# Five instead of four groups of seven-product blocks in the second product of the feed-forward layers, with the third products of three groups moved to the end

## Chip, cores and metric

The kernel runs on one core of one Trainium2 chip. The metric is the time of one execution in device microseconds; less is better. The input is 256 tokens of 1024 channels in float32.

## The reference

The reference is a trunk of two layers. Each layer has a feed-forward network (FFN), a mixer and a second FFN, each with an RMS norm ahead of it and a residual addition behind it:

```python
def swiglu(x, w_in, w_out):
    gate, up = jnp.split(x @ w_in, 2, axis=-1)
    return (jax.nn.silu(gate) * up) @ w_out
...
    for l in range(DEPTH):
        h = h + 0.5 * swiglu(rms_norm(h, ffn1_norm[l]), ffn1_w_in[l], ffn1_w_out[l])
        u = rms_norm(h, mix_norm[l])
        ...
        h = h + merged @ w_out[l]
        h = h + 0.5 * swiglu(rms_norm(h, ffn2_norm[l]), ffn2_w_in[l], ffn2_w_out[l])
    return rms_norm(h, final_norm)
```

The inner width of an FFN is 2816. The second product (by w_out) therefore sums over 22 k tiles of 128 channels, gives 1024 output columns (two halves n of 512) and has 256 tokens (two tiles t of 128). The mixer runs a Mamba-2 branch and a gated DeltaNet branch on one large projection. The change touches the mixer only in how and in what order some matmuls are issued, so the mixer's arithmetic is not shown here.

## The kernel before

**Weights.** All weights stream from HBM as tiles of 128x1024 float32 (512 KB). A tile lands in one of five buffers (`wraw`) by a DMA on SyncE's queue. ScalarE then makes its high part `whi` (line 67, type fp32r) and VectorE the rest `wlo` (line 70). A pair of `whi` and `wlo` is called a form; there are five buffers for each of the two. One float32 product is three matmuls: high by high, high by low, low by high (`mm3`, lines 317 to 320, and `mm3w`, lines 322 to 329). `take()` hands out the next form and issues loads and splits for the ones behind it; with `state["hold"]` set it issues no splits beyond the form that is asked for. The instructions are put in order on each engine at compile time by a scheduler that goes by priority, by readiness in its own model of time, and by free buffers, so an instruction can stand ahead of others that the source has before it. Within an engine the order is then fixed.

**The order of an FFN** is written as a string, `FFN` (line 37). "f" is the first chunk of the first product (four forms, 512-column matmuls). Each "c" is half of one of ten later chunks: two forms and 48 matmuls of 256 columns (`chan_chunk`). After two halves a chunk gives two k tiles of the gated activation: SiLU on ScalarE (tile `sg`), a product on VectorE (`g`), and the split into `gh` and `gl`.

**Block products.** Two k tiles, two token tiles and two column halves make a 2x2x2 block product, which takes seven block products instead of eight if sums of blocks are multiplied. A pair p stands for the k tiles 2p and 2p+1. On the side of the activations `block_sums` makes four sums per pair: four subtractions and additions, two high parts on ScalarE and two rests on VectorE (tiles `sf`, `bsa`, `bsb`, `bsc`, `bsd`). On the side of the weights the sums are made from tiles: `wsum` is loaded on SyncE's queue ("y" in the stream) into one of four slots, a second tile is added to it by an accumulating DMA on GpSimd's queue ("+"), then VectorE adds tiles (q0, q1), then another accumulating DMA follows (q3). `PAIRS` names four groups of two pairs, (1, 2) to (7, 8). "A" in the string is the four products of one group that go to four shared PSUM banks (tiles `p`, forms q1, q0, q2, q3; 24 matmuls). "B" is the three products that go straight to output banks (tiles `o`, forms q4, q5, q6; 18 matmuls). The third of these, q6, multiplies by the group's `wsum` and goes to the bank of token tile 1 and column half 0, so that the slot of the sum stays taken until then. `join` combines the shared banks and adds the results to the residual h by DMA. A "d" in the string is a direct k tile (`DIRECT`: 0, 1, 18 to 21): one form, 12 matmuls. The last five forms of a stage are direct ones, taken with `hold`; their matmuls for token tile 0 come first, so that the norm of that tile can run beside those of tile 1.

**Between stages.** `residual` adds o to h (line 392), `rms_chain` squares and sums on ScalarE (`junk`), takes the power on GpSimd (line 212), scales on VectorE (`hn`, by the norm vector `nw`), transposes on TensorE (`hnT`, line 284), and splits into `uW`, the input of the next stage (tile `t` in the mixer, `f` and `fc` in an FFN). This happens first for token tile 0 and then for tile 1. The norm vector has one buffer, `nw`, loaded by `norm_vec` at the start of an FFN. `out_chunks` multiplies the direct tiles in all three kinds of stages, and `close` ends the mixer with five forms in the same way.

**The cut.** `chan_chunk(ps, cut)` can write its fifth matmul as two of 128 columns (lines 324 to 326). It does so in the first half of the second chunk and in the half chunk after each "A". In the mixer no unit is cut. `ORDER` (lines 45 to 49) gives the order of the mixer's units, k1, k0, q1, k2, k3 first among those here.

## Time and profile before

| | |
|---|---|
| median of 3 runs | 1561.14 us (1560.59 to 1561.25) |
| the profiled execution's own time | 1561.29 us |
| its span | 1559.5 us |
| mean granted TensorE clock | 0.997 |
| busy: PE, DVE, ACT, POOL | 98%, 78%, 61%, 6% of the span |
| PE's share of the chain that ended last | 83% |

In the rows of the profile the start and the duration of instructions are in microseconds from the start of the span. PE is TensorE's matmul side and PEld its weight loads, DVE is VectorE, ACT is ScalarE, POOL is GpSimd, SP is SyncE; "out<-in" are the program's names of the tiles. A row of a window gives busy time with the number of instructions. The four FFNs follow each other at about 10, 602, 788 and 1374 us, and their second products on tiles o begin at 158, 747, 932 and 1519 us.

### The profile page before, as it was taken

To read this page: it belongs to the slowest core of one execution; us is meant where nothing else is said; L and a number is where in the kernel's file an instruction comes from. 1 tells how busy PE (TensorE), PEld (TensorE's weight loads), DVE (VectorE), ACT (ScalarE), POOL (GpSimd) and SP (SyncE) were. 2 spreads that over 40 slices of the span, in tenths; PEclk is the share of its full clock that TensorE was granted. 3 is DMA by queue.
4 is the path that set the end of the run, shared out by engine and by line. 5 is a ranking of instruction groups with operands and counts; after the bars stand their busy time and mean duration, and the time that the engine had idled before them with its cause. 6 is when DMAs were issued, how large, how long until landed. Compare 5 with 4: busy or idle time off the path is not lost.

```text
span 1559.5 us, 29036 instructions
## 1 busy us (share of the span) xinstructions
PE 1533.0 (98%) x11452; PEld 1387.0 (89%) x11452; DVE 1209.6 (78%) x1840; ACT 945.0 (61%) x1534; POOL 95.9 (6%) x108
## 2 busy tenths in 40 slices
PE   8999999999999999999999999999999999999998
PEld 7999879999888888999789998899998888889996
DVE  5778868967899766778677787699579996667786
ACT  5555667766665645556555566686756665455564
POOL 0000110000000000000100011000000000000010
PEclk9999999999999999999999999999999999999999
DMA  8877765553565585577966687655435547856784
GB/s 287 257 251 237 246 213 181 171 163 116 180 207 173 179 255 193 185 251 228 323 209 205 219 257 238 200 188 176 132 123 199 193 161 221 247 173 197 231 251 155
DMA packets 103438, 322.50 MB, mean 207 GB/s; under 512 B 23349, under 2 KB 24325, under 8 KB 102278
## 3 DMA queue, kind: packets, MB, share of 16 engines
q1 hardware_dynamic: 96390, 299.68, 57.0%
q0 software_dynamic: 6912, 20.97, 7.8%
q8 instruction: 90, 1.47, 0.4%
q14 instruction: 46, 0.38, 0.1%
HBM read 314.50 MB, written 1.92 MB: 203 GB/s over the span
## 4 chain that ended last, share of the span: by engine, by line
PE 83%; DVE 7%; DMA 3%; issue 3%; ACT 3%; POOL 1%; SPq 0%; POOLq 0%; ACTq 0%; DVEq 0%
PE fc L329 9%; PE fc L323 9%; PE fc L328 9%; DVE wlo L70 3%; PE t L319 3%; PE t L318 3%; PE t L320 3%; PE b L320 3%; PE b L319 3%; PE b L318 2%; PE o L320 2%; PE o L319 2%; PE o L318 2%; DMA wraw<-in_wst_dram 2%; PE p L319 2%
## 5 line engine op out<-in xcount | busy, mean ns | idle before, releaser
L70 DVE TENSOR_TENSOR wlo<-wraw,whi 128x1024 fp32r<-128x1024 f32 x504 | 611.1, 1221 | 174.5 <-ACT whi L67 166.9
L67 ACT ACTIVATE whi<-wraw 128x1024 fp32r<-128x1024 f32 x504 | 527.1, 1058 | 273.9 <-PE fc L328 87.7
L329 PE MATMUL fc<-uW,wlo 128*128 128x256 f32 x1280 | 354.8, 277 | 0.0
L323 PE MATMUL fc<-uW,whi 128*128 128x256 f32 x1280 | 354.1, 277 | 0.0
L328 PE MATMUL fc<-uW,whi 128*128 128x256 f32 x1260 | 348.2, 276 | 0.0
L323 PEld LDWEIGHTS fc<-uW,whi 128*128 128x128 f32 x1280 | 240.3, 188 | 0.8
L329 PEld LDWEIGHTS fc<-uW,wlo 128*128 128x128 f32 x1280 | 240.5, 188 | 0.0
L328 PEld LDWEIGHTS fc<-uW,whi 128*128 128x128 f32 x1260 | 236.5, 188 | 0.8
L318 PE MATMUL t<-whi,uW 128*128 128x512 f32 x256 | 102.0, 400 | 0.0
L319 PE MATMUL t<-wlo,uW 128*128 128x512 f32 x256 | 100.7, 393 | 0.6 <-DVE wlo L70 0.4
L320 PE MATMUL t<-whi,uW 128*128 128x512 f32 x256 | 100.8, 394 | 0.0
L318 PE MATMUL b<-whi,bh 128*128 128x512 f32 x192 | 76.3, 399 | 0.3 <-ACT bh L67 0.3
L319 PE MATMUL b<-wlo,bh 128*128 128x512 f32 x192 | 74.9, 390 | 0.0
L320 PE MATMUL b<-whi,bl 128*128 128x512 f32 x192 | 74.3, 394 | 0.6 <-DVE bl L70 0.6
L323 PE MATMUL xs<-uW,whi 128*128 128x256 f32 x256 | 72.6, 284 | 0.0
L329 PE MATMUL xs<-uW,wlo 128*128 128x256 f32 x256 | 71.1, 278 | 0.0
L328 PE MATMUL xs<-uW,whi 128*128 128x256 f32 x256 | 70.9, 277 | 0.0
L70 DVE TENSOR_TENSOR wlo<-wsum,whi 128x1024 fp32r<-128x1024 f32 x48 | 58.6, 1221 | 14.7 <-ACT whi L67 13.8
L67 ACT ACTIVATE whi<-wsum 128x1024 fp32r<-128x1024 f32 x48 | 50.8, 1058 | 28.4 <-PE fc L328 23.8
L318 PE MATMUL o<-whi,gh 128*128 128x512 f32 x160 | 63.8, 399 | 1.9 <-ACT whi L67 1.9
L319 PE MATMUL o<-wlo,gh 128*128 128x512 f32 x160 | 63.9, 399 | 1.6 <-DVE wlo L70 1.6
L165 POOL DMA_DIRECT2D wsum<-in_wst_dram x32 | 28.1, 878 | 584.3 <-DVE wlo L70 455.1
(320 smaller groups left out, 3429.8 us busy)
## 6 DMA issues: line engine op xcount, KB each, us to landing
wraw<-in_wst_dram SPq DMA_DIRECT2D x520, 512.0 KB, 5.0
wsum<-in_wst_dram POOLq DMA_DIRECT2D x32, 512.0 KB, 7.3
wsum<-in_wst_dram SPq DMA_DIRECT2D x16, 512.0 KB, 7.1
dc<-rdram SPq DMA_DIRECT2D x8, 1024.0 KB, 9.1
nw<-in_norms_dram SPq DMA_DIRECT2D x6, 512.0 KB, 6.3
h<-u POOLq DMA_DIRECT2D x12, 256.0 KB, 6.8
gb<-rdram SPq DMA_DIRECT2D x8, 256.0 KB, 5.7
h<-in_x_dram SPq DMA_DIRECT2D x4, 256.0 KB, 3.0
```

What stands on the lines that cost most here:

```text
L67: return A.activation(out=o, in_=i, func=func, **kw)
L70: return V.tensor_tensor(out=o, in0=a, in1=b, op=op)
L165: G.dma_start(out=r[:], in_=tile_of(i), accum_op=ALU.add)
L318: PE.matmul(ps, lh, rh, start=start, stop=False)
L319: PE.matmul(ps, lh, rl, start=False, stop=False)
L320: return PE.matmul(ps, ll, rh, start=False, stop=stop)
L323: PE.matmul(ps, wh, mh, start=start, stop=False)
L328: PE.matmul(ps, wh, ml, start=False, stop=False)
L329: PE.matmul(ps, wl, mh, start=False, stop=stop)
```

## The change

The groups become five, (0, 1) to (8, 9), so that 20 of the 22 k tiles are in block products, and the direct tiles are 20 and 21. The string of an FFN becomes "f", four times "cccc" and "A", "cc", "A", "cc", and "BBbbbddeee": "B" is a whole three products, "b" the first two of a group, and "e" the third product of a group whose first two came earlier. The groups take their turn in the order of `LATER`, 4, 0, 1, 2, 3. The fifth "A" comes straight after the chunk that makes pair 9. The sum tile of the fifth group lies in the buffer of the norm vector, which is therefore loaded later, after the first "B". The sums of pairs 8 and 9 lie in free columns of `gh` and `gl`. The k tiles 0 and 1 are copied from PSUM to SBUF ahead of their block sums. At the end come the two direct tiles, first for token tile 0, then for tile 1 with column half 1 ahead of half 0, and then three third products, which all go to tile 1, half 0. The residual addition and the square of tile 1 take half 1 first.

The parts that come from the sibling kernel: the low part of the third form of a next stage is placed behind the last residual addition (`state["late"]`); the five last forms of `close` take the last two k tiles for column half 0 and then for half 1; and the units k1, v2 and x20 of the mixer are cut.

```diff
-FFN = "f" + 8 * "c" + "A" + 4 * "c" + "A" + 4 * "c" + "A" + 2 * "c" + "A" + 2 * "c" + "BdBBBddddd"
-PAIRS = [(1, 2), (3, 4), (5, 6), (7, 8)]
-DIRECT = [0, 1, 18, 19, 20, 21]
+FFN = "f" + 4 * ("cccc" + "A") + "cc" + "A" + "cc" + "BBbbbddeee"
+PAIRS = [(0, 1), (2, 3), (4, 5), (6, 7), (8, 9)]
+LATER = [4, 0, 1, 2, 3]
+DIRECT = [20, 21]
@@ -107,23 +108,19 @@
         o, j2, begun, held = j + 4 * FC, j + 4 * FC + 22, [], []
-        spots, q = [], 0
-        for at, kind in enumerate(FFN):
-            if kind == "A":
-                spots.append(at - 2)
-        o1 = o + FFN[: FFN.index("A")].count("d")
+        later, last = list(LATER), list(LATER[FFN.count("B") :])
+        spots = [at - 2 for at, kind in enumerate(FFN) if kind == "A"]
         for at, kind in enumerate(FFN):
             if at in spots:
-                y = len(stream)
-                stream.extend([("y", o1 + 4 * q), ("+", o1 + 4 * q + 1, y)])
+                y, q = len(stream), len(begun)
+                stream.extend([("n" if q == 4 else "y", o + 4 * (q - len(held))), ("+", o + 4 * (q - len(held)) + 1, y)])
                 begun.append(y)
-                q += 1
             if kind in "fc":
                 j = plan_plain(j, 4 if kind == "f" else 2)
             elif kind == "d":
                 o = plan_plain(o, 1)
             elif kind == "A":
-                y, u = begun.pop(0), len(stream)
+                y, u = begun[len(held)], len(stream)
                 stream.extend([("w", o + 1), ("w", o + 2), ("w", o)])
                 plan.append(("q1", (y, u, u + 1), u + 2))
                 plan.append(("q0", (u + 2, y, u + 1), u + 3))
@@ -132,12 +129,15 @@
                 held.append((y, o + 2))
                 o += 4
             else:
-                y, b22 = held.pop(0)
-                stream.append(("w", b22))
-                plan.append(("q4", (len(stream) - 1,), len(stream)))
-                stream.append(("w", b22 + 1))
-                plan.append(("q5", (len(stream) - 1,), len(stream)))
-                plan.append(("q6", (y,), len(stream)))
+                if kind in "Bb":
+                    y, b22 = held[later.pop(0)]
+                    for i in range(2):
+                        stream.append(("w", b22 + i))
+                        plan.append((f"q{4 + i}", (len(stream) - 1,), len(stream)))
+                else:
+                    y, _ = held[last.pop(0)]
+                if kind in "Be":
+                    plan.append(("q6", (y,), len(stream)))
         return j2
 
     j0 = 0
...
+        elif kind == "n":
+            r = cpool.tile([P, D], F32, tag="nw", name="wsum")
...
                 tt(to, to, by, ALU.add)
+            if i in state["late"]:
+                behind.enter_context(tc.issue_after(state["late"].pop(i).ins))
             tt(lo[:], r[:], f(hi[:]), ALU.subtract)
...
         ss = small([P, 2], "ss")
-        for n in range(2):
+        for n in state["halves"]:
...
                 if add:
-                    add(t)
+                    added = add(t)
...
                 state["behind"][n + 4] = (state["square"].ins, ins.ins)
+                state["late"][n + 2] = added
...
             for t in range(2):
                 order = [(k, n) for n in range(2) for k in range(len(kk))]
                 if t == 1 and not split:
-                    order = [(k, n) for k in range(len(kk)) for n in range(2)]
+                    m = len(kk) - 2 if len(kk) == NSPL else len(kk)
+                    order = [(k, n) for k in range(m) for n in range(2)]
+                    order += [(k, n) for n in range(2) for k in range(m, len(kk))]
...
 
-    def residual(po, nw):
+    def residual(po, nw, first=0):
         def add(t):
-            for n in range(2):
+            state["halves"] = (first, 1 - first) if t == 1 else (0, 1)
+            for n in state["halves"]:
                 hv = h[:, t, n * 512 : (n + 1) * 512]
-                stt(hv, po[t][n][:], 0.5, hv, ALU.mult, ALU.add)
+                ins = stt(hv, po[t][n][:], 0.5, hv, ALU.mult, ALU.add)
+            return ins
...
 
-    def close_blocks(po, stat, sums, pb, nw):
-
-
-
-        direct, joined, n = list(DIRECT), join(pb), 0
-        rest = FFN[FFN.rindex("c") + 1 :]
-        for kind in rest[: len(rest) - NSPL]:
-            if kind == "d":
-                k = direct.pop(0)
-                out_chunks(po, stat, [k], None, first=k == DIRECT[0])
-                continue
+    def close_blocks(po, stat, sums, pb, nxt):
+
+        joined, nw, n_full = join(pb), None, FFN.count("B")
+
+        def third(p):
+            return stat(2 * p + 1, 1)
+
+        for n, q in enumerate(LATER):
             todo = [
-                (po[0][1], lambda p: sums(p, 3), PAIRS[n]),
-                (po[0][0], lambda p: stat(2 * p + 1, 0), PAIRS[n]),
-                (po[1][0], lambda p: stat(2 * p + 1, 1), PAIRS[n]),
+                (po[0][1], lambda p: sums(p, 3), PAIRS[q]),
+                (po[0][0], lambda p: stat(2 * p + 1, 0), PAIRS[q]),
+                (po[1][0], third, PAIRS[q]),
             ]
-            block_products(todo, n == 0, False)
-            n += 1
-            if n % 2 == 0:
+            block_products(todo if n < n_full else todo[:2], n == 0, False)
+            if n == 0 and nxt is not None:
+                nw = norm_vec(nxt)
+            if n < 2:
                 next(joined)
         state["hold"] = True
-        out_chunks(po, stat, direct, direct[-1], group=NSPL, split=nw is None, first=False)
-        return residual(po, nw)
+        ws = [(k, take()) for k in DIRECT]
+
+        def direct(t, n):
+            for k, (wh, wl) in ws:
+                sh, sl = stat(k, t)
+                c = slice(n * 512, (n + 1) * 512)
+                ins = mm3(
+                    po[t][n][:], sh, sl, wh[:, c], wl[:, c],
+                    k == DIRECT[0] and t == n == 1, k == DIRECT[-1] and (t, n) != (1, 0),
+                )
+                state["sums"].append(ins)
+
+        state["sums"] = []
+        for n in range(2):
+            direct(0, n)
+        state["sums"] = []
+        for n in (1, 0):
+            direct(1, n)
+        for q in LATER[n_full:]:
+            state["sums"] += block_products([(po[1][0], third, PAIRS[q])], False, q == LATER[-1])
+        return residual(po, nw, 1)
...
         bsc = slots.tile([P, 4, 2, P], F32R, tag="sI", name="bsc")
-        bsd = s2.tile([P, 2, 2, P], F32R, tag="s2", name="bsd")
+        bsd, bse = (g[2][:, 6:8].rearrange("p i (o t) -> p i o t", o=2) for g in (gl, gh))
...
 
-            q, i = (p - 1) // 2, (p - 1) % 2
+            q, i = p // 2, p % 2
             if j < 3:
                 b = (bsa[:], bsb3)[q % 2]
                 return b[:, i, 0, j, :], b[:, i, 1, j, :]
-            b = (bsc[:, 0:2], bsc[:, 2:4], bsb1, bsd[:])[q]
+            b = (bsc[:, 0:2], bsc[:, 2:4], bsb1, bsd, bse)[q]
...
                             PE.transpose(bank[:, k * S + t * P : k * S + (t + 1) * P], gt[t][:, k * P : (k + 1) * P], ident)
-                    split(0, bank[:].rearrange("p (k t) -> p k t", k=2))
+                    g0 = tmp2("g2")
+                    act(g0[:], bank[:])
+                    split(0, g0[:].rearrange("p (k t) -> p k t", k=2))
+                    block_sums(0, g0)
...
             ps = accb("kk")
-            chan_chunk(ps)
+            chan_chunk(ps, hp == 1)
...
             ps = accb("vv")
-            chan_chunk(ps)
+            chan_chunk(ps, hp == 2)
...
             ps = accb("xs")
-            chan_chunk(ps)
+            chan_chunk(ps, (g, i) == (2, 0))
...
     for l in range(DEPTH):
-        ffn(norm_vec(3 * l + 1))
+        ffn(3 * l + 1)
         mixer(l, norm_vec(3 * l + 2))
-        add = ffn(norm_vec(3 * l + 3) if l + 1 < DEPTH else None)
+        add = ffn(3 * l + 3 if l + 1 < DEPTH else None)
```

8 lines of the change are left out of this document (5 added, 3 removed).

## Prediction

> **What bounds the kernel now.** I read the page first.
>
> ```profile
> span 1559.5 us, 29036 instructions
> PE 1533.0 (98%) x11452; PEld 1387.0 (89%) x11452; DVE 1209.6 (78%) x1840; ACT 945.0 (61%) x1534; POOL 95.9 (6%) x108
> q1 hardware_dynamic: 96390, 299.68, 57.0%
> q0 software_dynamic: 6912, 20.97, 7.8%
> ```
>
> TensorE is busy in 98% of the span, so matmuls set the time, and only fewer matmuls, a faster pace or the removal of the remaining waits can help. The mean duration of a matmul is no price, because matmuls overlap; the price is the length of a row of them. I took the stages of the second product (tiles p and o) by windows and restricted them to their tile. Columns: window, length, then busy time and count of each engine, granted clock, DMA share, GB/s.
>
> ```profile
> core 0: us, PE busy (x) PEld busy (x) DVE busy (x) ACT busy (x), PEclk, DMA share, GB/s
> 659.30:664.76 5.46, 5.43 (x24) 4.36 (x24) 0.00 (x0) 0.00 (x0) 1.00 0.57 103
> 158.18:189.12 30.94, 30.50 (x132) 24.45 (x132) 1.38 (x2) 0.00 (x0) 1.00 0.84 259
> 747.02:784.00 36.98, 33.85 (x132) 26.14 (x132) 1.38 (x2) 0.00 (x0) 0.91 1.01 308
> 932.45:962.38 29.93, 29.91 (x132) 24.62 (x132) 1.38 (x2) 0.00 (x0) 1.00 0.78 240
> ```
>
> Twenty-four matmuls of 512 columns take 5.46 us, so one is worth 0.2275 us. In the third FFN 132 of them on o take 29.93 us, which is the same pace with no wait. The first FFN loses 1.0 us there, and the second loses 7.05 us (36.98 - 29.93) at a DMA share of 1.01. That one stage is the largest wait of the kernel. The DMA issues in it show why:
>
> ```profile
> wraw<-in_wst_dram SPq DMA_DIRECT2D x13, 512.0 KB, 9.5
> wsum<-in_wst_dram SPq DMA_DIRECT2D x4, 512.0 KB, 8.7
> wsum<-in_wst_dram POOLq DMA_DIRECT2D x4, 512.0 KB, 8.9
> ```
>
> Thirteen ordinary weight tiles share the engines with four sum tiles and four accumulating transfers. These sum tiles belong to the next FFN: their four slots come free as the groups finish, and the loads are hoisted into this stage. Weight tiles then land after a median of 9.5 us.
>
> **The change, part by part.**
>
> *Fewer matmuls.* A pair of k tiles costs 24 matmuls directly and 21 as block products. Pairs (0, 1) to (8, 9) replace (1, 2) to (7, 8), that is eight pairs become ten, and six direct tiles become two: 8x21 + 6x12 = 240 matmuls become 10x21 + 2x12 = 234. Six fewer in each of four FFNs are 24 x 0.2275 = 5.4 us off the engine that sets the time: **-5.4 us**.
>
> *The cuts in the mixer.* Matmuls of 256 columns run at two paces. The same five units (k1, k0, q1, k2, k3: 240 matmuls) stand here for layer 0 and then layer 1, and then v2 to the middle of the b units for both layers:
>
> ```profile
> 233.20:261.55 28.35, 28.35 (x242) 28.35 (x242) 25.30 (x54) 20.93 (x37) 0.00 (x0) 1.00 0.59 197
> 1006.12:1033.43 27.31, 27.31 (x242) 27.31 (x242) 24.99 (x54) 20.61 (x36) 0.00 (x0) 1.00 0.61 203
> 307.38:332.30 24.92, 24.92 (x212) 24.80 (x210) 17.60 (x35) 11.18 (x15) 0.00 (x0) 1.00 0.52 139
> 1079.26:1104.20 24.94, 24.94 (x212) 24.80 (x210) 17.88 (x37) 11.49 (x15) 0.00 (x0) 1.00 0.51 141
> ```
>
> Equal work takes 28.35 us and 27.31 us, so 118 ns against 114 ns for one matmul. The v stretches run at 24.92/212 = 118 ns, the slow pace, in both layers. In the FFNs the first chunk after the existing cut runs on at the fast pace. If a cut sets the fast pace here too, k1 is worth 1.04 us in layer 0 and nothing in layer 1 (fast already), and v2 is worth 24.92 x (1 - 27.31/28.35) = 0.9 us in each layer. The cut at x20 precedes only a short stretch, and I put it at 0.1 us in each layer. What a cut costs is seen in the first one of the kernel:
>
> ```profile
> 38.04 0.28 PE L323 MATMUL fc<-uW,whi 128*128 128x256 f32 x1
> ...
> 38.49 0.28 PE L323 MATMUL fc<-uW,whi 128*128 128x256 f32 x1
> ```
>
> Three ordinary starts of 0.118 us would take 0.35 us and these took 0.45 us, so six cuts cost 0.6 us. Sum 1.04 + 1.8 + 0.2 - 0.6: **-2.5 us**; bounds -3.1 and +0.6 (no change of pace).
>
> *Third products kept for the end.* Groups 1 to 3 keep their sum tiles until the five last forms. So of the four slots only that of group 0 is free for the next FFN during this stage, and of the eight extra transfers above about two remain. The next FFN's others move into its own first stage. I take 5.5 of the 7.05 us as saved: **-5.5 us**, bounds -7 and 0. Against it, the stage becomes denser: 132 + 12 matmuls with 18 forms become 114 with 17, and the three "b" groups take two loads and two splits per 12 matmuls, 2.7 us. At the page's 1.22 us for the DVE's part of a split, that is 2.44 us of 2.7. I put **+1.5 us** for the four FFNs, bounds 0 and +7 (the second FFN's loss, once more).
>
> *The added vector work.* Each FFN gets three more splits (1.22 us on DVE, 1.06 us on ACT each), two additions of weight tiles (1.2 us) and two sets of block sums (about 2 us), so some 10 us of DVE, and four more loads of 512 KB. The rows:
>
> ```profile
> L70 DVE TENSOR_TENSOR wlo<-wraw,whi 128x1024 fp32r<-128x1024 f32 x504 | 611.1, 1221 | 174.5 <-ACT whi L67 166.9
> L67 ACT ACTIVATE whi<-wraw 128x1024 fp32r<-128x1024 f32 x504 | 527.1, 1058 | 273.9 <-PE fc L328 87.7
> 904.00:921.00 17.00, 17.00 (x125) 15.94 (x125) 14.82 (x20) 10.61 (x14) 0.86 (x1) 1.00 0.85 256
> ```
>
> The densest existing stretch, two half chunks and a group, has DVE busy in 14.82 of 17 us and TensorE without a gap. The change uses this pattern once and four half chunks per group, which is looser, four times. I cost the work at nothing while matmuls cover it; without cover it would be 40 us. In the first FFN, however, the first group now comes after four half chunks (some 22 us) instead of eight, so five sum tiles crowd into the kernel's start: **+1 us**, bounds 0 and +5.
>
> *The fifth group's wait.* This is the one new wait. Groups so far use pairs whose sums were made at least one chunk earlier. The fifth uses pair 9, which is made from the chunk that ends just before it. Two samples of this chain, from the last matmul of a chunk to the high halves of its sums (the ACT row on bsa or bsb), lightly loaded and then loaded:
>
> ```profile
> 626.46 0.28 PE L329 MATMUL fc<-uW,wlo 128*128 128x256 f32 x1
> 629.99 0.53 ACT L67 ACTIVATE bsa<-sf 128x384 fp32r<-128x384 f32 x1
> 714.07 0.39 PE L318 MATMUL p<-whi,bsa 128*128 128x512 f32 x1
> 715.17 0.36 ACT L67 ACTIVATE sg<-fc 128x256 f32<-128x256 f32 x1
> 720.74 0.51 ACT L67 ACTIVATE bsb<-sf 128x384 fp32r<-128x384 f32 x1
> ```
>
> The group would begin 0.11 us after 626.46, and the sums are there at 630.52, so 3.95 us later. In the loaded sample it is 721.25 - 714.07 = 7.2 us. Pair 8 offers 12 matmuls without pair 9, 2.7 us, if the compile-time order puts them first. The wait is 3.95 - 2.7 = 1.2 us, up to 7.2 - 2.7 = 4.5 us, or 7.2 - 0.7 = 6.5 us if pair 9 stands second as in the source; matmuls of the next chunk could fill it down to 0. I take 1.7 us, close to the quick sample, because while the four forms of the group are held, hardly any later splits can be put between the links of the chain. Behind the waiting matmul stands all that TensorE still has, so it counts in full. Four times: **+6.8 us**, bounds 0 and +26.
>
> *Transitions.* The last n half of token tile 1 now needs one residual addition and one square after the final matmul, not two. The transition as it is:
>
> ```profile
> 193.64 1.28 DVE L73 SCALAR_TENSOR_TENSOR h<-o,h 128x512 f32<-128x512 f32 x2
> 196.32 0.55 POOL L212 TENSOR_TENSOR zz<-zz,mhalf 128x1 f32<-128x1 f32 x1 [8.65 <-DVE zz L78]
> 197.71 0.66 PE L284 MATMUL hnT<-cs,hn 128*128 128x128 f32 x4 [0.89 <-DVE hn L73]
> PE hnT L284 <- DVE hn L73: 5.3, 6, 1.0
> ```
>
> The chain from 193.64 to 197.71 gets shorter by about 0.64 us, but TensorE has ready matmuls to run meanwhile, and its 5.3 us in six waits arise since the transposes are placed earlier than they can run. If the order moves with the chain, nothing is gained. The d forms are freed only 18 matmuls before the end, which can delay the next stage's first two splits. I take -0.2 us for each of five: **-1 us**, bounds -2.5 and +3. The load of the next norm vector waits for group 4's tile, but 66 matmuls (15 us) still cover its landing.
>
> *Sum.* -5.4 - 2.5 - 5.5 + 1.5 + 1 + 6.8 - 1 = -5.1 us. The profiled execution took 1561.29 us (its span and 1.8 us around it), 0.15 us above the median of 1561.14. The forecast is 1561.1 - 5.1 = **1556.0 us**.
>
> **The clock.** A long wait costs more than itself. In the second FFN's slow stage:
>
> ```profile
> 768.00:773.60 5.60, 2.52 (x6) 0.82 (x5) 2.45 (x2) 2.04 (x2) 0.00 (x0) 0.83 1.05 276
> 773.60:778.50 4.90, 4.87 (x12) 3.81 (x13) 0.69 (x1) 0.72 (x2) 0.86 (x1) 0.50 1.03 366
> ```
>
> After 5.6 us with six matmuls the granted clock is 0.50, and twelve matmuls take 4.9 us instead of 2.7, so 2.2 us are added. The Trainium skill (TensorE: Matmul & The Clock Gate, Part 1) says that one idle window of about 3.4 us brings the clock back to half, and its closing table advises no idle gaps above some 3 us. By that rule the waits of 1.7 us that I forecast leave the clock alone, and waits of 6.5 us halve it. The trace agrees on the halving, but here it came without one wholly idle window, since six matmuls ran in the 5.6 us.
>
> **Rivals.** *Slower: the fifth group waits long.* At 4.5 us for each FFN the sum is -5.1 + 4 x (4.5 - 1.7) = +6.1, so 1567.2 us. At 6.5 us and 2.2 us of slow clock it is 4 x 8.7 - 11.9 = +22.9, so 1584 us. It decides from 11.9/4 = 3.0 us per FFN on, and from 3.75 us it shows as slower. For it: the loaded sample, and transposes that already stand too early in the order. Against it: the group holds four of the five buffers, so the chain meets few other splits. *Faster: the wait is covered.* With 0 in place of 6.8 the time is 1549.2 us, and with the best transitions 1547.7. For it: next-chunk matmuls are ready, and in the trace matmuls do stand out of source order. *No change: the loads stay.* If the slow stage keeps its 7 us because the denser loads replace the hoisted ones, the time is 1556.0 + 5.5 = 1561.5 us. For it: four more loads per FFN. Against it: the third FFN, whose stage moves 240 GB/s without a wait. *The cuts do nothing:* 1556.0 + 3.1 = 1559.1 us.
>
> **How the numbers follow.** Chances: forecast 0.36 (with its own range 1553 to 1559.5), covered wait 0.24, long wait 0.24, loads stay 0.12, idle cuts 0.04. A measurement of this kernel can tell about 0.2%, 3.1 us. Faster by more than that, below 1558.0: 0.28 of the forecast's 0.36, the covered wait's 0.24 and 0.02 of the loads, 0.54. Within: 0.08, 0.07 and the idle cuts' 0.03, 0.18. Slower: the long wait's 0.24, 0.03 and 0.01, 0.28. The range runs from 1547 (covered wait, best transitions) to 1567 (the long wait at 4.5 us); what lies outside is the upper part of the long wait and a few cases of several gains at once.
>
> **What would show it.** Right: 24 fewer matmuls on p and o; the slow stage near 114 x 0.2275 = 26 us; v units at 114 ns; in each FFN one gap of 1 to 3 us on p before pair 9, ended by ACT or DVE on bsa. Wrong: gaps there of over 4 us or a clock below 1 beside them; a DMA-ended wait in the b groups; the paces of the mixer unchanged.

## Result and profile after

The changed kernel takes 1579.71 us (median, 1574.93 to 1581.47) against 1560.87 us (1559.89 to 1561.25) for the kernel before, run beside it: a ratio of 1.0116, 95% interval 1.0104 to 1.0129. The forecast was 1556.0 us, faster; the change is slower by 18.8 us. The profiled execution is the fastest of the four (1574.93 us, span 1572.7), so what follows accounts for +13.2 us of span.

First the page of the kernel after, the lines that answer to those of before:

```profile
span 1572.7 us, 29116 instructions
PE 1535.8 (98%) x11438; PEld 1381.3 (88%) x11438; DVE 1238.8 (79%) x1908; ACT 955.6 (61%) x1566; POOL 107.0 (7%) x116
q1 hardware_dynamic: 97542, 303.87, 58.3%
q0 software_dynamic: 8064, 25.17, 9.1%
```

GpSimd's queue (q0) moves 25.17 MB, not 20.97: eight accumulating transfers of 512 KB more. TensorE's busy time grows by 2.8 us only, so most of the loss is time in which it stands. VectorE's grows by 29.2 us and still fills only 79% of the span. I took the length of each FFN from the start of its first matmul on f to that of the next stage. FFN 1 to 4 changed by +7.4, -3.0, +8.3 and +4.7 us, the two mixers by -3.1 and -0.5, the start by -0.8. The second FFN, where the forecast put its gain, did gain. The others lost more. The waits of TensorE in the kernel after (total, times, longest):

```profile
PE hnT L288 <- DVE hn L74: 5.8, 10, 1.2
PE p L324 <- DVE wlo L71: 4.8, 10, 0.8
PE fc L334 <- DVE wlo L71: 4.1, 8, 1.0
...
PE p L323 <- ACT gh L68: 1.7, 4, 0.4
...
PE fc L328 <- ACT whi L68: 1.5, 1, 1.5
```

The waits on p and fc are new, and most of their time ends with a split of a weight tile. Two places hold most of them.

**The fifth group.** Windows of the kernel after, from the first matmul of the fifth group to the end of the last chunk, for the four FFNs: 24 matmuls on p and 97 on fc. In the kernel before, its last group and the two half chunks behind it take 16.5 us, without a gap:

```profile
149.67:170.24 20.57, 18.34 (x124) 15.74 (x122) 18.16 (x26) 11.82 (x17) 2.86 (x4) 1.00 0.83 252
739.34:759.56 20.22, 18.34 (x124) 15.74 (x122) 17.76 (x26) 11.49 (x16) 2.80 (x4) 1.00 0.84 246
927.18:945.81 18.63, 17.78 (x124) 15.90 (x122) 16.47 (x24) 10.54 (x14) 3.02 (x4) 1.00 0.90 280
1517.83:1538.39 20.56, 18.39 (x123) 15.74 (x122) 18.26 (x26) 11.71 (x16) 2.99 (x4) 1.00 0.85 254
```

TensorE's waits in the second of them, on its timeline:

```profile
740.70 0.50 PE L324 MATMUL p<-wlo,gh 128*128 128x512 f32 x1 [0.28 <-DVE wlo L71]
741.84 0.50 PE L324 MATMUL p<-wlo,bsa 128*128 128x512 f32 x1 [0.17 <-DVE wlo L71]
743.63 0.50 PE L324 MATMUL p<-wlo,bsa 128*128 128x512 f32 x1 [0.83 <-DVE wlo L71]
744.76 0.39 PE L334 MATMUL fc<-uW,wlo 128*128 128x256 f32 x1 [0.17 <-DVE wlo L71]
745.76 0.50 PE L323 MATMUL p<-whi,gh 128*128 128x512 f32 x1 [0.43 <-ACT gh L68]
```

The excess is 4.1, 3.7, 2.1 and 4.1 us, 14.0 in all. In the second FFN these rows name 1.9 us of 3.7; the rest lies in longer distances between the starts around the waits, and 0.4 us in a slower pace of the last 92 matmuls. Only the last wait, 0.43 us, is for pair 9. The others are for splits of weight tiles, the first three in the part that works on pair 8. VectorE has 17.76 us of work in these 20.22, so it is close behind. What it had waited for shows on its own timeline, then on GpSimd's, then in the DMA issues of 726 to 733 us (count, KB each, median us to landing):

```profile
735.89 1.23 DVE L71 TENSOR_TENSOR wraw<-wraw 128x1024 f32<-128x1024 f32 x1 [2.69 <-DMA wraw<-in_wst_dram]
737.03 1.22 DVE L71 TENSOR_TENSOR wlo<-wsum,whi 128x1024 fp32r<-128x1024 f32 x1
```

```profile
726.75 0.86 POOL L165 DMA_DIRECT2D wsum<-in_wst_dram  x1 [27.07 <-DVE wlo L71]
```

```profile
wraw<-in_wst_dram SPq DMA_DIRECT2D x4, 512.0 KB, 8.0
wsum<-in_wst_dram POOLq DMA_DIRECT2D x1, 512.0 KB, 8.9
```

At 726.75 GpSimd issues the accumulating transfer for the third product of the fourth group. It needs 8.9 us. The weight tiles issued just behind it take 8.0 us, and two of them are the operands of the fifth group's first addition on VectorE. VectorE was done with its earlier work at 733.2 us (735.89 - 2.69) and stood before that addition until 735.89, and the four splits of the group come behind it, one after the other. A wait of that length is not new: in front of the groups two to four of this FFN VectorE waits 3.00, 2.56 and 2.83 us for the same kind of tile. But there its addition begins 8.7 to 9.7 us ahead of the group's first matmul, and here 3.45 us ahead (735.89 against 739.34).

**The head of the third FFN.** The second stretch of fc of FFN 3 in windows (all of it, then its two last parts), TensorE's gaps in it, and the DMA issues from 777 to 812 us:

```profile
806.43:828.60 22.17, 19.01 (x148) 18.41 (x147) 13.09 (x23) 9.85 (x17) 0.89 (x1) 0.92 0.70 231
820.00:824.00 4.00, 1.75 (x11) 1.35 (x10) 3.43 (x6) 2.88 (x5) 0.00 (x0) 0.93 0.44 132
824.00:828.60 4.60, 4.60 (x30) 4.60 (x30) 4.53 (x10) 3.45 (x7) 0.00 (x0) 0.69 0.75 219
```

```profile
818.85 0.39 PE L334 MATMUL fc<-uW,wlo 128*128 128x256 f32 x1 [0.91 <-DVE wlo L71]
821.75 0.39 PE L328 MATMUL fc<-uW,whi 128*128 128x256 f32 x1 [1.49 <-ACT whi L68]
823.02 0.39 PE L334 MATMUL fc<-uW,wlo 128*128 128x256 f32 x1 [0.76 <-DVE wlo L71]
```

```profile
wraw<-in_wst_dram SPq DMA_DIRECT2D x11, 512.0 KB, 10.4
wsum<-in_wst_dram SPq DMA_DIRECT2D x5, 512.0 KB, 9.0
wsum<-in_wst_dram POOLq DMA_DIRECT2D x5, 512.0 KB, 11.8
```

The same 145 matmuls take 16.54 us in FFN 4, so 5.6 us are lost here. All five sum tiles and their accumulating transfers stand together, and ordinary tiles take 10.4 us. In the kernel before, the loads of this FFN's sum tiles stood in the closing stage of FFN 2. FFN 1 loses 2.5 us in the same way.

**The closing stages.** Windows on tile o of FFN 1, 2 and 3, and the one large wait in the second:

```profile
170.24:199.43 29.19, 26.76 (x114) 20.98 (x114) 1.87 (x3) 0.00 (x0) 1.00 0.81 248
759.56:788.26 28.70, 26.54 (x114) 21.00 (x114) 1.88 (x3) 0.00 (x0) 1.00 0.99 326
945.81:974.98 29.17, 26.77 (x114) 20.98 (x114) 1.88 (x3) 0.00 (x0) 1.00 0.79 244
```

```profile
784.35 1.32 PE L288 MATMUL hnT<-cs,hn 128*128 128x128 f32 x8 [0.89 <-DVE hn L74]
```

The second stage has lost its 7 us: 28.70 us, as the others. 114 matmuls are 25.9 us of that, the transposes 1.3, and gaps most of the rest.

**The mixer.** Windows over k1 to k3, then v2 to the middle of the b units, each for layer 0 and layer 1:

```profile
238.51:265.94 27.43, 27.43 (x243) 27.43 (x243) 25.45 (x54) 21.23 (x35) 0.00 (x0) 1.00 0.60 189
1014.48:1041.89 27.41, 27.41 (x243) 27.41 (x243) 24.04 (x52) 20.15 (x35) 0.00 (x0) 1.00 0.57 184
311.78:335.83 24.05, 24.05 (x213) 23.92 (x211) 17.19 (x35) 10.29 (x13) 0.00 (x0) 1.00 0.54 144
1087.53:1112.46 24.93, 24.93 (x212) 24.80 (x211) 18.73 (x40) 11.50 (x15) 0.00 (x0) 1.00 0.55 146
```

k1 of layer 0 now runs at the fast pace, and so does v2 there. In layer 1 v2 is slow as before, although the v unit ahead of it now runs at the fast pace (113.8 ns for a matmul, 117.6 behind the cut).

### The profile page after: what moved, and what is told of

It reads as the page before. It is cut to its first block, busy times and chain, and to the rows that moved or that the text cites. A ratio compares the mean times of both kernels' runs of the same rounds, so it can differ in the third digit from the quotient of the medians.

```text
span 1572.7 us, 29116 instructions
## 1 busy us (share of the span) xinstructions
PE 1535.8 (98%) x11438; PEld 1381.3 (88%) x11438; DVE 1238.8 (79%) x1908; ACT 955.6 (61%) x1566; POOL 107.0 (7%) x116
## 3 DMA queue, kind: packets, MB, share of 16 engines
q0 software_dynamic: 8064, 25.17, 9.1%
## 5 line engine op out<-in xcount | busy, mean ns | idle before, releaser
L68 ACT ACTIVATE gh<-g 128x512 fp32r<-128x512 f32 x44 | 27.9, 633 | 104.0 <-DVE g L71 103.3
L165 POOL DMA_DIRECT2D wsum<-in_wst_dram x40 | 35.1, 885 | 599.5 <-DVE wlo L71 463.6
L71 DVE TENSOR_TENSOR wlo<-wsum,whi 128x1024 fp32r<-128x1024 f32 x60 | 72.4, 1218 | 0.1
L71 DVE TENSOR_TENSOR wraw<-wraw 128x1024 f32<-128x1024 f32 x20 | 24.5, 1225 | 59.2 <-DMA wraw<-in_wst_dram 59.2
L68 ACT ACTIVATE whi<-wsum 128x1024 fp32r<-128x1024 f32 x60 | 62.2, 1049 | 4.2 <-PE fc L333 2.7
```

Source lines behind the costliest of these rows:

```text
L68: return A.activation(out=o, in_=i, func=func, **kw)
L71: return V.tensor_tensor(out=o, in0=a, in1=b, op=op)
L165: G.dma_start(out=r[:], in_=tile_of(i), accum_op=ALU.add)
```

## Experiments

Each was timed beside the kernel before, whose median in these rounds was 1560.1 to 1562.3 us.

**The changed kernel again**, unedited.

> The changed kernel once more, unaltered, for its spread and a second trace. Theory A (three places: the fifth group's wait, 14 us in the first trace; sum tiles that crowd the head of the first and third FFN, 8 us; the transposes of token tile 0, 3 us): the same three places show again, 1575 to 1581 us, and what differs from 1574.9 us lies in waits for weight tiles. Theory B (the added vector work and loads as a whole starve TensorE, spread over each FFN): waits on splits all along the chunks.

1583.29 us, ratio 1.0141 (1.0124 to 1.0159). The loss stands.

**Parts of the change alone.** First the sibling's changes on the kernel before (three cuts, the order of the last two tiles, the late low part), then only the three cuts.

```diff
-            chan_chunk(ps)
+            chan_chunk(ps, hp == 1)      # k; hp == 2 for v, (g, i) == (2, 0) for x
...
+            if i in state["late"]:       # first kernel only, with the order in out_chunks
+                behind.enter_context(tc.issue_after(state["late"].pop(i).ins))
```

> The kernel before with the sibling's part alone: cuts at k1, v2 and x20, the low part of the third form behind the last residual addition, and the last two of five forms by column half; four groups as before. Theory A: cuts 2 us, transitions 0.3 to 0.5 us at each of five, together 3 to 5 us less than before, about 1557 us. Rival (the transposes move with the chain and cuts only sometimes set the pace): 0 to 1.5 us less.

> The kernel before with the three cuts in the mixer alone. If a cut sets the fast pace wherever it stands: k1 in layer 0 and v2 in both layers, 2 to 2.5 us less than before. If it only shifts the phase, a unit that was fast may turn slow: 0.5 to 1.5 us less, and the rest of the sibling's 3.7 us is the transitions'.

1557.63 us, ratio 0.9974 (0.9961 to 0.9987), and 1560.12 us, 0.9992 (0.9983 to 1.0001). The sibling's part gains about 4 us; the cuts alone are too near to no change to be told. So the loss lies in the rest of the change, in the FFNs.

**The fifth group later.** Behind the last chunk; then also taken last in the closing stage.

```diff
-FFN = "f" + 4 * ("cccc" + "A") + "cc" + "A" + "cc" + "BBbbbddeee"
+FFN = "f" + 5 * ("cccc" + "A") + "BBbbbddeee"
...
-LATER = [4, 0, 1, 2, 3]
+LATER = [0, 1, 2, 3, 4]      # second kernel; its "n" tile is then that of group 0
```

> The fifth group comes after the tenth chunk instead of the ninth, so the sums of pair 9 have a whole chunk (11 us) to be made; loads, splits and matmuls are as many. Theory A: the p stretches of the fifth group take 5.5 us without a gap and the last chunk runs at the fast pace; 12 to 14 us less than the changed kernel, about 1565 us. Theory B: at most 4 us less, and the waits on splits turn up in the following o stage.

> As the kernel with the fifth group after the tenth chunk, but the groups take their turn in order 0 to 4, so that the first B no longer needs the sum tile whose accumulating transfer has just been issued; group 0 lies in the norm vector's buffer instead of group 4. Theory C (the fifth group's products and then its sum tile are each needed before they are ready; both waits are of position, not of capacity): chunks and p as short as in that kernel (137.5 to 141 us), the o stages back from 37.5 to about 30 us, 7 us less per FFN, about 1570 us. Theory B (DMA and vector work as a whole are short there): o stages of 35 us or more, over 1588 us.

1599.69 us, ratio 1.0244 (1.0225 to 1.0263), and 1578.28 us, 1.0107 (1.0093 to 1.0121); neither time was expected. In the first, the gaps on p go and larger ones come on o: the group's third product is wanted at once, and its accumulating transfer had only just been issued.

```profile
PE o L323 <- ACT whi L68: 22.5, 7, 6.2
```

The second takes that wait away and ends where the change was: o stages of 33 us, and FFN 3's head still losing 6.8. A place for the group alone is no cure.

**Sum loads in the order of the source**, each behind the load ahead of it.

```diff
-        state["last"] = nc.sync.dma_start(r[:], tile_of(i))
+        with ExitStack() as order:
+            if kind in ("y", "n") and state["last"] is not None:
+                order.enter_context(tc.issue_after(state["last"].ins))
+            state["last"] = nc.sync.dma_start(r[:], tile_of(i))
```

> Each load of a sum tile is placed behind the weight load before it in the source, so it can't be hoisted to the end of the stage before. Theory A: the third FFN's first chunks lose their wait of 5.6 us and the first FFN's part of its 2.5 us; 5 to 8 us less than the changed kernel. Rival (DMA bandwidth as such is short there): the wait stays or moves, 0 to 2 us less.

1612.57 us, ratio 1.0325 (1.0304 to 1.0345), outside both expectations. FFN 3's head lost its gaps, but now the sums themselves came late (waits of the kernel on TensorE and VectorE):

```profile
PE fc L337 <- DVE wlo L71: 20.8, 15, 3.6
```

```profile
DVE wraw L71 <- DMA wraw<-in_wst_dram: 118.0, 20, 9.2
```

VectorE's time in front of the groups' first additions rose from 59.2 us (20 times) to 118.0.

**Third products early again**, with five groups.

```diff
-FFN = "f" + 4 * ("cccc" + "A") + "cc" + "A" + "cc" + "BBbbbddeee"
+FFN = "f" + 4 * ("cccc" + "A") + "cc" + "A" + "cc" + "BBBBBdd"
```

> The changed kernel with all five third products in their groups (BBBBBdd), none kept for the end; then only 12 matmuls of token tile 1 follow token tile 0. Theory A (the sum slots held to the end push the next FFN's sum loads into its head): the third FFN's head loses most of its 5.6 us, the second FFN's o stage gets 4 to 7 us longer as before, and each transition gets 2 to 4 us longer for want of cover. Net 5 to 12 us slower than the changed kernel. Rival (the thirds at the end are what costs): faster than the changed kernel.

1583.7 us, ratio 1.0145 (1.0131 to 1.0158). The changed kernel gave 1.0116 and 1.0141 in its two timings. The second stretch of fc in FFN 3 is free (0.4 us), but the transposes wait longer, 4.6 us of it once the third FFN has begun:

```profile
PE hnT L288 <- DVE hn L74: 14.5, 13, 4.6
```

The second FFN's closing stage does not fall back: its 114 matmuls on o take 25.9 us without a gap, and with the transposes and the wait for them the stage takes 29.7 us, against 28.7 in the changed kernel. So keeping the third products for the end makes a difference of 1 to 5 us, hardly more than the two timings of the changed kernel differ by: what it gains at the transitions it gives back at the head of the next FFN.

**Sum loads bounded**: a sum tile may be loaded at most ten (in the second and third kernel eight) weight loads early. On the sibling's part, on the kernel with the fifth group last, and on the changed kernel.

```diff
+            if kind in ("y", "n") and len(issued) >= 10:
+                order.enter_context(tc.issue_after(issued[-10].ins))
...
+        if kind == "w":
+            issued.append(state["last"])
```

> The sibling's part alone (four groups), with each load of a sum tile placed behind the weight load ten loads before it, so that it can run ahead by ten loads at most. Theory A (sum tiles hoisted from the next FFN cause the 7 us of the second FFN's o stage): that stage falls from 41.6 to 34 us, the third FFN's chunks stay at 131.8 us; about 7 us less than the sibling's part, 1550 us. Rival (the weight tiles alone are short of bandwidth there): the stage stays over 38 us.

> The kernel of groups 0 to 4 with the fifth after the tenth chunk, and sum loads bounded in the same way (eight loads). Theory A: the third FFN's head, 4.5 to 5.8 us of waits, is free of them, chunks and p near 138 us in each FFN; 4 to 6 us less than without the bound. If the sums then come late, waits ended by VectorE on wlo or wsum appear in front of the first groups instead and the gain is under 2 us.

> The changed kernel with each load of a sum tile placed behind the weight load eight loads before it. Theory A: the waits at the head of the first and the third FFN (2.6 and 5.8 us in its first trace) go, the fifth group's wait of 2 to 4 us in each FFN stays; 8 to 12 us less than the changed kernel, 1568 to 1575 us. Rival (what the bound gives with the other order of groups comes from that order): 0 to 4 us less.

1549.62 us, ratio 0.9925 (0.9911 to 0.9939); 1566.1 us, 1.0037 (1.0023 to 1.0051); 1578.41 us, 1.0106 (1.0088 to 1.0123). With four groups this is the fastest complete kernel of the study: 8 us below the sibling's part, as the second FFN's closing stage falls from 41.6 to 34.5 us. With the changed kernel it missed the expectation. The heads are free, but VectorE waits longer in front of additions, and TensorE behind it (waits of the third kernel, one engine and then the other). The bound has a price of its own: the transfer into the fifth sum tile, which in the changed kernel's second FFN was issued by 615.74, now stands together with that of the third group at 703.43, ahead of the fourth group's addition, which waits 8.05 us instead of 2.83.

```profile
DVE wraw L71 <- DMA wraw<-in_wst_dram: 75.9, 20, 8.1
```

```profile
PE p L329 <- DVE wlo L71: 9.1, 12, 1.4
```

**Pair 9 or the transfers?** Two edits to the last kernel, one by one and both: the group takes pair 8's sums for pair 9's; the accumulating transfers of weights are left out.

```diff
-                    (pb[5], lambda p: sums(p, 0), PAIRS[n]),
+                    (pb[5], lambda p: sums(min(p, 8), 0), PAIRS[n]),   # and the other three
...
         if kind == "+":
-            add_to(raws[stream[j][2]], i)
             return
...
-        if kind == "q3":
-            add_to(r, js[1])
```

> The same, but the fifth group's four products take pair 8's activations and sums for pair 9 as well (this part of the computation is changed); the sums of pair 9 are still made, and matmuls, splits and loads are as many. Theory A (the wait is for pair 9's sums alone): the p stretch of the fifth group runs in 5.5 us, and the time falls by 8 to 14 us against the run beside it, to about 1561 us. Rival (the splits of the group's own forms are what is late, by vector work and loads): half of the wait or more stays, at most 6 us less.

> The changed kernel with bounded sum loads, and without the accumulating transfers of weight tiles (40 in the kernel; the sum tiles then hold one tile only, so this part of the computation is left out). VectorE's and ScalarE's work and the order of the matmuls are untouched; 20 MB of transfers go. Theory 1 (the fifth group and the dense last stage lose time because weight tiles land late, the accumulating transfers being the slowest part of that traffic): the waits on splits of late tiles go (9.1 us on p, 3.0 us on fc, 1.7 us on o in the kernel with bounded sums), 1563 to 1568 us against its 1578. Theory 2 (the wait is for the vector work on pair 9 and the group's own two additions, and transfers only ride along): the p waits stay, 1574 to 1578 us.

> Both at once: the fifth group takes pair 8's sums in place of pair 9's, and the accumulating transfers of weight tiles are left out (both parts of the computation are changed). With pair 9 not awaited but the transfers kept, the group of 24 matmuls ran without a gap and the saving came back as waits of the next stage for splits (o 28.1 and 29.8 us in the first two FFNs at 102 matmuls of 23.2). Theory 1 (supply of weight tiles is what binds the last 60 us of an FFN): those waits go too, and the two costs together are 16 to 22 us, 1555 to 1561 us. Theory 2 (VectorE's and ScalarE's work in that stretch is what binds): the next stage keeps its waits, 1570 to 1576 us.

| us (ratio, interval) | transfers kept | left out |
|---|---|---|
| pair 9 awaited | 1578.41 (1.0106, 1.0088 to 1.0123) | 1554.61 (0.9954, 0.9937 to 0.997) |
| not awaited | 1576.59 (1.01, 1.0081 to 1.0119) | 1550.31 (0.9928, 0.991 to 0.9945) |

The wait for pair 9 is worth 2 to 4 us in the whole kernel, hardly more than the intervals, and the transfers 24 to 26. Leaving the transfers out also spares the splits of the sum tiles their wait for them, so it does not yet tell how they cost. Without pair 9 the group does run without a gap, and the closing stage takes it back, 33.7 us in place of 29.4 (windows of that kernel: the fifth group with its half chunks, then tile o of the second FFN):

```profile
740.75:757.27 16.52, 16.52 (x123) 15.44 (x122) 12.68 (x19) 9.23 (x13) 0.86 (x1) 1.00 0.88 270
757.27:790.98 33.71, 28.20 (x114) 20.67 (x114) 1.88 (x3) 0.00 (x0) 1.00 0.84 249
```

**Four groups in the same arrangement**: half chunks, cuts, transitions and late third products (of two groups) as changed, with bounded sum loads.

```diff
-FFN = "f" + 4 * ("cccc" + "A") + "cc" + "A" + "cc" + "BBbbbddeee"
+FFN = "f" + 4 * ("cccc" + "A") + "cccc" + "BBbbddddddee"
-PAIRS = [(0, 1), (2, 3), (4, 5), (6, 7), (8, 9)]
+PAIRS = [(0, 1), (2, 3), (4, 5), (6, 7)]
...
+        for k in DIRECT[:-2]:
+            out_chunks(po, stat, [k], None, first=k == DIRECT[0])
```

> The changed kernel with bounded sum loads but four groups, pairs (0, 1) to (6, 7), and six direct k tiles, four of them ahead of the closing stage; groups after every fourth half chunk, third products of two groups kept for the end, cuts and transitions as changed. 240 matmuls in place of 234 in each FFN, so 5.4 us more TensorE work. Theory 1 (the fifth group behind two half chunks is what costs): no wait before the last group, 1547 to 1554 us, below the kernel before in spite of the extra matmuls. Theory 2 (the groups' closer spacing, the crowded head of the FFN and the late third products cost by themselves): 1562 us or more.

1551.29 us, ratio 0.9934 (0.9918 to 0.995), with 24 matmuls more than the changed kernel. VectorE's wait in front of additions is 39.0 us in 16, as before the change (37.2 in 16). The closer spacing and the late third products cost next to nothing (1.7 us above the sibling's part with bounded loads); the fifth group does.

**Which transfers, and is it their place?** With bounded sum loads, two of each FFN stand ahead of the fifth group: into its sum tile, and for the fourth group's third product. They are left out; then all are held by one group; then the two are put behind VectorE's additions.

```diff
+            if stream[stream[j][2]][0] == "y":           # first kernel, and q3 of group 4
                 add_to(raws[stream[j][2]], i)
...
+        if kind == "q2" and state["adds"]:               # second kernel
+            add_to(*state["adds"].pop())
...
+            with tc.issue_after(two.ins):                # third kernel, at q0
+                while state["adds"]:
+                    add_to(*state["adds"].pop())
```

> The changed kernel with bounded sum loads, without two accumulating transfers in each FFN: that into the fifth group's sum tile and that of the fourth group's third product... both issued shortly ahead of the fifth group (8 of 40; this part of the computation is left out). Leaving out all 40 gave 1554.6 against 1578.4 us. Theory 1 (those ahead of the last two groups do it): over half of the gain, 1560 to 1567 us. Theory 2 (the gain is in proportion to the traffic): 8/40 of 23.8 us, 1572 to 1575 us.

> The changed kernel with bounded sum loads; the accumulating transfer that prepares a group's third product is issued one group later, after the additions of the next group, since it is only needed in the closing stage (the fifth group's at once, as before). Same work and transfers, so only their place changes. Theory 1 (the transfers issued just ahead of a group delay its two tiles for VectorE's first addition, behind which all of VectorE's queue stands: idle 8.1 us before the fourth group and 3.8 us before the fifth in the second FFN): VectorE's idle time on weight tiles falls from 75.9 us to about 45, and 1578 us become 1560 to 1568. Theory 2 (the load of the engines as a whole binds, wherever it stands): 1574 us or more, since the transfers then fall on the fifth group or the closing stage.

> The changed kernel with bounded sum loads; the accumulating transfer into the fifth group's sum tile is issued behind the fourth group's second addition on VectorE, and that of the fourth group's third product behind the fifth group's second addition. Both so far stand ahead of the additions behind which they now are. All work and all 40 transfers are kept. (Holding each transfer by one whole group, as in the run before, only put it where its neighbour had stood.) Theory 1 (place: these two transfers delay the two tiles of VectorE's first addition in the fourth and fifth groups): VectorE's idle time on weight tiles falls from 75.9 us to 45 to 60, and the time from 1578 to 1558 to 1568 us. Theory 2 (traffic as a whole in the last 60 us of an FFN): the waits reappear in the fifth group and the closing stage, 1572 us or more.

1554.37 us, ratio 0.9957 (0.9945 to 0.9969): these eight of forty are worth as much as all. The other two gave 1577.97 us, 1.0091 (1.0074 to 1.0109), and 1577.22 us, 1.0111 (1.0094 to 1.0128), but tell nothing on place: GpSimd's queue has its transfers at the same places as without the edits. In the second kernel each held transfer stands where its neighbour stood; in the third `issue_after` names an instruction of another engine, and no order on the chip came of it. The timeline of GpSimd in the third kernel still has a pair of transfers ahead of the fourth group and one ahead of the fifth:

```profile
698.89 1.75 POOL L165 DMA_DIRECT2D wsum<-in_wst_dram  x2 [14.32 <-issue]
725.95 0.86 POOL L165 DMA_DIRECT2D wsum<-in_wst_dram  x1 [25.30 <-DVE wlo L71]
```

The last run moves them by the order within one queue: the fifth sum tile is loaded behind the fourth group's last weight tile on SyncE, and the fourth group's transfer goes behind the fifth's on GpSimd. All forty are kept.

```diff
+            back = 1 if kind == "n" else 8
+            if kind in ("y", "n") and len(issued) >= back:
+                order.enter_context(tc.issue_after(issued[-back].ins))
...
+            if state["group"] == 4:
+                state["adds"].append((r, js[1]))
+            else:
+                with tc.issue_after(add_to(r, js[1]).ins):
+                    while state["adds"]:
+                        add_to(*state["adds"].pop())
```

> The changed kernel with bounded sum loads, all 40 accumulating transfers kept, two of each FFN moved within their queues: the fifth group's sum tile is loaded behind the fourth group's last weight tile (seven loads later than in the kernel with bounded sums), so that its accumulating transfer follows the fourth group's loads; and the accumulating transfer for the fourth group's third product stands behind that of the fifth group on GpSimd's queue. The compiled order has them there; in the two runs before it had left all of them where they were. Theory 1 (place): VectorE's idle time before the first addition of the fourth and fifth groups in the second FFN (8.1 and 3.8 us) falls to below 3 us each, the waits of p for splits fall from 9.1 us to below 4, and the kernel takes 1558 to 1568 us. Theory 2 (traffic): the moved transfers hold up the fifth group or the closing stage instead, 1573 us or more.

1557.5 us, ratio 0.9975 (0.9964 to 0.9987): 20.9 us less than with bounded sum loads alone, with the same work and traffic. Its GpSimd timeline, VectorE's first additions of the fourth and fifth groups, the DMA issues of 722 to 729 us (where the fifth group's tiles are among them):

```profile
711.98 0.86 POOL L165 DMA_DIRECT2D wsum<-in_wst_dram  x1 [17.61 <-DMA wsum<-in_wst_dram]
736.31 1.76 POOL L165 DMA_DIRECT2D wsum<-in_wst_dram  x2 [23.46 <-DVE wlo L71]
```

```profile
708.96 1.23 DVE L71 TENSOR_TENSOR wraw<-wraw 128x1024 f32<-128x1024 f32 x1 [3.08 <-DMA wraw<-in_wst_dram]
...
728.34 1.22 DVE L71 TENSOR_TENSOR wraw<-wraw 128x1024 f32<-128x1024 f32 x1
```

```profile
wraw<-in_wst_dram SPq DMA_DIRECT2D x4, 512.0 KB, 4.9
```

With no transfer ahead of them the tiles land in 4.9 us instead of 8.0, the fifth group's addition waits for nothing, and no wait on p or fc is left in the list of TensorE's waits. VectorE's wait in front of additions falls from 75.9 us to 41.8. From the first matmul of the fifth group to the end of the last chunk, the second FFN takes 21.65 us with bounded loads alone and 17.32 us here (one window of each kernel):

```profile
742.34:763.99 21.65, 18.61 (x123) 15.73 (x122) 19.35 (x27) 12.99 (x18) 2.99 (x4) 1.00 0.82 247
734.78:752.10 17.32, 17.24 (x124) 15.91 (x123) 13.34 (x19) 10.40 (x14) 2.62 (x3) 1.00 1.00 283
```

Over 16.5 us, the four FFNs lose 20.6 us there with bounded loads alone and 3.3 us here. The two moves were not tried singly, and not without the bound, so how much of the changed kernel's own 14.0 us they would save was not measured.

## Why the prediction was wrong

**The step that failed** is "I cost the work at nothing while matmuls cover it", together with "This is the one new wait". The added work was priced as VectorE time and compared with a dense stretch that ran well (14.82 of 17 us). VectorE's time alone was not the problem: the run with two transfers moved does the same work without a wait of p or fc. What failed is the assumption that the work's operands are there in time. The stretch that I took as a model has the same pattern, a group two half chunks behind another and GpSimd's transfer for the earlier group's third product ahead of it (kernel before, third FFN):

```profile
901.17 0.86 POOL L165 DMA_DIRECT2D wsum<-in_wst_dram  x1 [26.83 <-DVE wlo L70]
908.50 1.23 DVE L70 TENSOR_TENSOR wraw<-wraw 128x1024 f32<-128x1024 f32 x1 [0.87 <-DMA wraw<-in_wst_dram]
```

There the transfer landed after 6.9 us, and the addition waited 0.87 us and still began 7.5 us ahead of the group's first matmul at 915.99. In the second FFN of the changed kernel the transfer took 8.9 us, the two tiles behind it 8.0, and the addition waited 2.69 us and began 3.45 us ahead. VectorE itself came to it 2.2 us later than in the model (6.1 us ahead of the group instead of 8.4); in the last run it came 6.4 us ahead, found its tiles, and nothing waited. Since the order of VectorE's instructions is fixed, the splits behind the addition wait with it. Why the same transfer takes 8.9 us here and 6.9 us there stays open. The prediction named "four more loads of 512 KB", but followed none of them to the instruction that waits for it.

**The fifth group's wait** was put at 6.8 us, 1.7 for each FFN. It measured 14.0 us, within the bounds of 0 to 26, but by another mechanism. The chain from pair 9's chunk to its sums is covered by pair 8's matmuls and five of the next chunk's, almost as the rival of a covered wait had it: 0.4 us is left, in each FFN. Part of that cover was the delay itself, since pair 8's twelve matmuls took 4.9 us instead of 2.7. In the last run, where they are not delayed, the stretch exceeds 16.5 us by 0.8 us in each FFN, so the term would have been 3.3 us. The mark that I gave, "one gap of 1 to 3 us on p before pair 9, ended by ACT or DVE on bsa", did not appear; the gaps are ended by wlo. The rival "the fifth group waits long" gave the right sign for a wrong reason. Its price of 4.5 us is close to the 3.5 us measured, but making pair 9's sums unnecessary gained 2 us in the kernel with bounded loads, whose fifth groups lose 20.6. About 0.4 us of the excess is neither wait: the last 92 matmuls on fc run at 118 ns. They do so in the two kernels where matmuls on p stand between the two halves of their cut (changed, last run), and at 113 ns where none does (before, pair 9 not awaited); that this is the cause was not tested.

**Third products at the end**, -5.5 us: the stage gained all of its 7 us. Of its eight extra transfers not two remain, as forecast, but six, and they stand in its last 11 us (777 to 788) instead of from its start on. That early sum loads slow it is shown by the sibling's part with bounded loads (41.6 to 34.5 us). But the run with early third products keeps the gain, so the late ones were not needed for it; what took the wait away there is open. And "The next FFN's others move into its own first stage" was said and not priced. It cost 5.6 us in FFN 3; FFN 1 lost 2.5 us (put at 1, bounds 0 to 5).

**Fewer matmuls**, -5.4 us: 114 on o in place of 132 + 12, and 120 on p in place of 96. The run with four groups, which lacks this gain, is nevertheless 6 us faster than the best arrangement with five.

**Denser closing stage**, +1.5 us for the kernel: the b groups ran nearly clean in the changed kernel. In the kernel without waits at the fifth group (the last run) o waits 0.8, 1.2 and 0.6 us for splits in the closing stages of FFN 1 to 3, 2.6 us in all, so the term was somewhat small, within its bounds of 0 to 7. **Transitions**, -1 us: ten waits on hnT of 5.8 us in place of six of 5.3, so no gain with five groups; in the sibling's part alone these waits fell to 3.1 us. **The cuts**, -2.5 us: layer 0 as forecast, layer 1 not; the run with the cuts alone allows 0 to 3 us, and there v2 runs at the fast pace in both layers.

**The clock.** The waits at the fifth group left the granted clock at 1.00, as forecast for waits of 1.7 us. In FFN 3's head three waits of 0.91, 1.49 and 0.76 us in 5.1 us brought it to 0.69 for the next 4.6 us. The Trainium skill (TensorE: Matmul & The Clock Gate, Part 1) ties the fall to an idle window of about 3.4 us; here, as in the kernel before, it came without a wholly idle one.

## What to carry to other kernels

An added step has a price in operands as well as in engine time. Follow each new load to the instruction that needs it, see which transfers are issued within one landing time ahead of it, how far ahead of its user that instruction begins, and what stands behind it on its engine. Where a wait is removed and the time stays, look upstream for the supply: a two by two of the suspected wait and the suspected supply tells them apart in four runs. And look at the compiled order of a queue before reading a result as a test of place.

## Not expected of the hardware

An accumulating transfer of 512 KB took 5.4 to 18.0 us from issue to landing, with a median of 7.3 us in the kernel before and 8.9 us in the changed one, where an ordinary load of the same size took 5.0 and 5.2 us. Ordinary tiles issued just behind one needed 8.0 us, and 4.9 us where none stood ahead. Two transfers of each FFN, issued one landing time too early, cost the kernel with bounded sum loads 20.9 us. Cutting one matmul of 256 columns in two can change the pace of those behind it, but does not fix which pace follows: in the changed kernel v2 of layer 0 went from 24.92 to 24.05 us, while in layer 1 v2 still took 24.93 us behind the same cut.
